# Block products of four feed-forwards: two more raw weight buffers, and rounds of 4, 6, 6, 6 chunks

## The chip, the cores and the metric

The kernel runs on one core of a Trainium2 chip. The metric is the device time of one execution in microseconds; the figure of a kernel is the median of its runs, and less is better. Everything is computed in float32 accuracy: each float32 operand is split into a rounded high part H and a remainder L, and a product takes three matmuls (H by H, H by L, L by H).

## The reference

Two transformer blocks in a row, each of two layers, on one sequence of 512 tokens of width 1024. Each layer holds a mixer (dilated attention, gated linear attention, a latent attention with a short convolution) and one or two gated feed-forwards. The change touches the feed-forwards only:

```python
def swiglu(h, w_gate_up, w_down):
    g, u = jnp.split(h @ w_gate_up, 2, axis=-1)
    return (jax.nn.silu(g) * u) @ w_down
```

Here `h` is 512 x 1024, `w_gate_up` is 1024 x 5632, `w_down` is 2816 x 1024. There are six such feed-forwards in the program.

## The kernel before

A feed-forward (`ffn`, L472) cuts the 2816 hidden columns into 22 chunks of 128 and works through them in rounds. A round computes its chunks (gate, up, silu, product, split into `gH` and `gL`) and then a down phase: for four pairs of output blocks `m`, all chunks of the round times `w_down`, added to the residual `x` by VectorE (`x_add`, L408). Two of the six feed-forwards use plain matmuls (`ffn_up`, L518). The other four, called fast here, are the ones of the change. In them chunks 0 to 3 are plain, and from chunk `FAST` = 4 on each chunk is a block product (`ffn_fast`, L618): the 1024-deep product of one gate and one up column block with two halves of the tokens is done with seven half-size products in place of eight, 84 matmuls of 256 columns a chunk, and five additions of the products on VectorE (L626, `s<-...`), the product of the halves (L648) and the split of the result (`gL`).

The weights of a block product are prepared by a chain (`fast_w`, L582) that runs one chunk ahead. It takes two raw loads of 512 KB (each two DMAs of 256 KB), a left one (rows 0 to 511: `a11`, `a21`) and a right one (rows 512 to 1023: `a12`, `a22`), and makes four sums on GpSimd (L588, tile `sr`, s1 to s4), of which the first needs the right load and the last, s4, is the last reader of the right load. ScalarE casts and VectorE subtracts to split `a11` and the four sums (`swH`, `swL`) and the whole right load (`wh`, `wl`, four buffers).

All raw loads of the program, left, right and those of the plain and the down weights, go into one tag with three buffers:

```python
raw = self.wp.tile([P, kc, n], F32, tag="wraw", name=self.nm("wraw"), bufs=3)
```

The list of loads is fixed in advance (`ffn_specs`, L439), the loader stands four entries ahead of the use (`AHEAD` = 3, `pop_ahead`), and all loads go through SyncE's queue, which issues them in order: a load that waits for its buffer holds those behind it. The order of the instructions on each engine is made by the compiler's scheduler; each engine then runs its list strictly in order. At the end of the plain chunks, `ffn_up` also starts `fast_h` (L545), which makes the sums of the token halves, tiles `ta` and `tb`.

PSUM has three `mm` banks, two `sc` and one `o`, and a bank is given out again when its last reader is done.

Of the kernel before, what the change touches and what calls it, by code (L numbers as in the profile page):

```python
# [8 lines left out]
F32 = mybir.dt.float32  # L9
# [7 lines left out]
P = 128  # L17
S = 512
D = 1024
NC = D // P  # L20
NT = S // P
FF = 2816
# [19 lines left out]
OWN = [("ada", 3)] * 3 + [("adacc", 2)] * 2 + [("lw", 3)] * 3  # L42
FFN_CUTS = ((0, 6), (6, 16))

FAST_CUTS = ((0, 6), (6, 8), (14, 8))
FAST = 4
OWN += [("taH", 1), ("taL", 1), ("tbH", 1), ("tbL", 1)]
HALF = (slice(0, S // 2), slice(S // 2, S))
# [154 lines left out]
class Net:  # L203
# [140 lines left out]
    def wload(self, name, layer, r0, kc, c0, n, own=None):  # L344

        nc = self.nc
        raw = self.wp.tile([P, kc, n], F32, tag="wraw", name=self.nm("wraw"), bufs=3)
        if isinstance(c0, tuple):

            b = n // 2  # L350
            for i in range(2):
                src = self.A[name][layer, r0:r0 + kc * P, c0[i]:c0[i] + b].rearrange("(k p) n -> p k n", p=P)
                nc.sync.dma_start(raw[:, :, i * b:(i + 1) * b], src)
        else:
            src = self.A[name][layer, r0:r0 + kc * P, c0:c0 + n].rearrange("(k p) n -> p k n", p=P)
            nc.sync.dma_start(raw, src)
        if own == "raw":
            return raw
        if own is None:
            H = self.wp.tile([P, kc, n], F32R, tag="wh", name=self.nm("wh"), bufs=4)  # L360
            L = self.wp.tile([P, kc, n], F32R, tag="wl", name=self.nm("wl"), bufs=4)
        else:
            H, L = (self.tile(t, [P, kc, n], F32R, b) for t, b in OWN[2 * own:2 * own + 2])
        self.split(H, L, raw)
        return [(H[:, k], L[:, k]) for k in range(kc)]
# [77 lines left out]
    @staticmethod  # L443
    def ffn_specs(wgu, wdn, l, fast=False):
        for j0, nj in FAST_CUTS if fast else FFN_CUTS:
            for j in range(j0, j0 + nj):
                if fast and j >= FAST:
                    if j == FAST:
                        yield from Net.fast_specs(wgu, l, j)
                    yield from Net.fast_specs(wgu, l, j + 1)  # L450
                elif j % 2 == 0:
                    for part in range(2):
                        for k in range(0, NC, 4):
                            yield wgu, l, k * P, 4, part * FF + j * P, 2 * P
            for m in range(0, NC, 2):
                yield from Net.down_specs(wdn, l, j0, nj, m, fast)

    @staticmethod
    def fast_specs(wgu, l, j):

        return [(wgu, l, k * P, 4, (j * P, FF + j * P), 2 * P, "raw") for k in range(0, NC, 4) if j < FF // P]

    @staticmethod
    def down_specs(wdn, l, j0, nj, m, fast=False):
# [4 lines left out]
    def ffn(self, pre, wgu, wdn, l, coef, norm, begin=None, ada=False, fast=False):  # L469

        with self.phase(4):
            self.g_bufs = 8 if fast else 16  # L472
            for j0, nj in FAST_CUTS if fast else FFN_CUTS:
                last = j0 + nj == FF // P
                gs = []
                for j in range(j0, j0 + nj):
                    if fast and j >= FAST:
                        gs.append(self.ffn_fast(wgu, l, j))
                    elif j % 2 == 0:
                        gs += self.ffn_up(pre, wgu, l, j, fast and j + 2 == FAST)  # L480
                    if j == 0:
                        if begin is not None:
                            with self.tc.issue_after(self.ahead):
                                begin()
                        self.ada_on = True
                if last:
                    self.ada_on = ada
                for m in range(0, NC, 2):
                    specs = list(self.down_specs(wdn, l, j0, nj, m, fast))
                    if last and m == NC - 2:  # L490
                        self.ada_on = False
                        if ada:
                            self.ada_on = True
                            self.until(lambda: self.ada.done)
                            self.ada_on = False
                        self.until(lambda: not self.ada_open)
                        parts = [self.part(*s) for s in specs]
                        for half in range(2):
                            ps = [self.bank(("mm", "sc")[half], [P, S // 2]) for _ in range(2)]
                            self.pairs(ps, parts, gs, HALF[half])  # L500
                            for i in range(2):
                                self.x_add(m + i, ps[i], coef, norm, half)
                            norm.finish(half)
                        norm.wait(0)
                    else:
                        ps = [self.bank(("mm", "sc")[m // 2 % 2], [P, S]) for _ in range(2)]
                        self.pairs(ps, self.parts(specs), gs)
                        for i in range(2):
                            self.x_add(m + i, ps[i], coef, norm if last else None)
# [1441 lines left out]
```

## Time and profile before

| | before |
|---|---|
| median of 3 runs | 3761.65 us (3760.25 to 3763.08) |
| the profiled execution: time, and span of its instructions | 3759.42 us, 3757.6 us |
| mean granted TensorE clock | 0.978 |
| busy share: TensorE matmul, weight load, VectorE, ScalarE, GpSimd | 95%, 84%, 67%, 42%, 18% |
| mean DMA rate over the span | 102 GB/s |

In the rows, PE is TensorE (PEld its weight loads), DVE is VectorE, ACT ScalarE, POOL GpSimd, SP SyncE; `mm<-hH,swH` names the tile written and the tiles read, buffer numbers left out. Idle time stands in square brackets or behind the bar, with the instruction that ended it. The clock column is the share of TensorE's full clock that was granted.

The four fast feed-forwards run their block products at about 1393 to 1680, 2393 to 2680, 2780 to 3068 and 3407 to 3697 us of the span.

### The profile page before, as it was taken

What the parts mean: (1) busy time and instruction counts of PE and PEld (TensorE: products, weight loads), DVE (VectorE), ACT (ScalarE), POOL (GpSimd) and SP (SyncE); (2) the same over time, 40 slices, a digit from 0 to 9 for tenths busy, and PEclk for the clock granted to TensorE, in tenths of its full rate; (3) what the DMA queues carried; (4) which work ended last, traced back from release to release, by engine and by line L of the source; (5) the groups of instructions that cost most, each with busy time, mean ns of one, the idle gap of its engine ahead of it and who ended that gap; (6) DMA issues with size and microseconds to landing.
All of it is one profiled execution on the core that took longest, in us unless ns stands there. A gap on an engine that the chain in (4) does not pass through costs nothing.

```text
span 3757.6 us, 55731 instructions
## 1 busy us (share of the span) xinstructions
PE 3585.0 (95%) x21654; PEld 3168.1 (84%) x21654; DVE 2505.6 (67%) x4331; ACT 1571.0 (42%) x2960; POOL 690.9 (18%) x532
## 2 busy tenths in 40 slices
PE   9999999999999989999999999899989999998998
PEld 7878788888888978888888888788888888887888
DVE  7676667786546676666765478775677566777765
ACT  5545455422236543343222355443443334543433
POOL 3111211000001133230000000342133220013431
PEclk9999999999999989999999999999999999999999
DMA  4122121286432223324764221233313232213232
GB/s 128 57 68 63 51 69 61 84 283 223 152 87 66 75 62 96 101 85 162 264 226 132 75 90 57 73 90 96 112 58 101 90 102 83 76 50 98 79 101 74
DMA packets 402625, 384.98 MB, mean 102 GB/s; under 512 B 19626, under 2 KB 375480, under 8 KB 402360
## 3 DMA queue, kind: packets, MB, share of 16 engines
q1 hardware_dynamic: 402360, 381.42, 32.2%
q8 instruction: 170, 2.79, 0.3%
q14 instruction: 95, 0.78, 0.1%
HBM read 379.26 MB, written 2.10 MB: 101 GB/s over the span
## 4 chain that ended last, share of the span: by engine, by line
PE 76%; DVE 9%; DMA 5%; issue 5%; ACT 3%; POOL 2%; SPq 0%; ACTq 0%; POOLq 0%; DVEq 0%
PE mm L230 46%; PE sc L230 21%; PE o L230 4%; DVE swL L322 3%; PE sm L230 2%; DMA wraw<-in_ffn_w_down 2%; DMA wraw<-in_ffn_w_gu 2%; PE pt L230 2%; DVE wl L322 1%; ACT wh L321 1%; POOL sr L588 1%; DVE s L551 1%; DMA wraw<-in_ffn_w_gate_up 1%; DMA ada<-in_w_ada 1%; DVE s L626 1%
## 5 line engine op out<-in xcount | busy, mean ns | idle before, releaser
L322 DVE TENSOR_TENSOR wl<-wraw,wh 128x1024 fp32r<-128x1024 f32 (+2 forms) x501 | 605.0, 1210 | 438.7 <-ACT wh L321 428.1
L321 ACT CAST wh<-wraw 128x1024 fp32r<-128x1024 f32 (+2 forms) x501 | 508.3, 1019 | 820.3 <-PE mm L230 286.6
L230 PE MATMUL mm<-hL,wh 128*128 128x512 f32 (+1 forms) x1288 | 441.2, 346 | 2.2 <-DVE hL L129 1.8
L230 PE MATMUL mm<-hH,wl 128*128 128x512 f32 (+1 forms) x1288 | 439.6, 346 | 0.0
L230 PE MATMUL mm<-hH,wh 128*128 128x512 f32 (+1 forms) x1288 | 426.8, 348 | 13.3 <-ACT hH L128 11.2
L230 PE MATMUL mm<-wh,hH 128*128 128x512 f32 (+1 forms) x896 | 318.4, 358 | 3.1 <-ACT hH L321 1.7
L230 PE MATMUL mm<-wh,hL 128*128 128x512 f32 (+1 forms) x896 | 316.4, 354 | 0.0
L230 PE MATMUL mm<-wl,hH 128*128 128x512 f32 (+1 forms) x896 | 313.8, 353 | 1.5 <-DVE wl L322 1.5
L230 PEld LDWEIGHTS mm<-hH,wh 128*128 128x128 f32 x1288 | 235.2, 190 | 45.1 <-ACT hH L128 13.1
L230 PEld LDWEIGHTS mm<-hL,wh 128*128 128x128 f32 x1288 | 245.4, 191 | 31.2 <-DVE hL L129 2.2
L322 DVE TENSOR_TENSOR swL<-sr,swH 128x512 fp32r<-128x512 f32 x288 | 262.9, 923 | 12.6 <-ACT swH L321 11.5
L230 PEld LDWEIGHTS mm<-hH,wl 128*128 128x128 f32 x1288 | 245.6, 191 | 29.3
L385 POOL TENSOR_TENSOR rs<-rs,mhalf 128x2 f32<-128x2 f32 (+1 forms) x26 | 22.3, 858 | 1271.8 <-DVE rs L384 1271.8
L230 PE MATMUL sc<-hH,wl 128*128 128x512 f32 (+1 forms) x688 | 237.3, 349 | 0.0
L230 PE MATMUL sc<-hL,wh 128*128 128x512 f32 (+1 forms) x688 | 237.1, 349 | 0.0
L321 ACT CAST swH<-sr 128x512 fp32r<-128x512 f32 x288 | 173.2, 618 | 131.7 <-PE mm L230 79.7
L230 PE MATMUL sc<-hH,wh 128*128 128x512 f32 (+1 forms) x688 | 226.8, 350 | 0.0
L230 PE MATMUL mm<-gH,wh 128*128 128x512 f32 x528 | 208.8, 400 | 12.7 <-ACT wh L321 9.3
L588 POOL TENSOR_TENSOR sr<-wraw,wraw 128x512 f32<-128x512 f32 x72 | 100.9, 1402 | 647.6 <-DMA wraw<-in_ffn_w_gu 382.3
L230 PE MATMUL mm<-gH,wl 128*128 128x512 f32 x528 | 209.8, 398 | 3.9 <-DVE wl L322 3.9
L230 PE MATMUL mm<-hH,swH 128*128 128x256 f32 x576 | 167.8, 293 | 45.8 <-DVE s L626 45.8
L230 PE MATMUL mm<-gL,wh 128*128 128x512 f32 x528 | 208.6, 395 | 0.0
(518 smaller groups left out, 9862.7 us busy)
## 6 DMA issues: line engine op xcount, KB each, us to landing
ada<-in_w_ada SPq DMA_DIRECT2D x144, 512.0 KB
wraw<-in_ffn_w_gu SPq DMA_DIRECT2D x216, 256.0 KB
wraw<-in_ffn_w_down SPq DMA_DIRECT2D x96, 512.0 KB
wraw<-in_ffn_w_gu SPq DMA_DIRECT2D x68, 512.0 KB
wraw<-in_a_w_in SPq DMA_DIRECT2D x128, 256.0 KB
wraw<-in_ffn_w_gate_up SPq DMA_DIRECT2D x52, 512.0 KB
wraw<-in_ffn_w_down SPq DMA_DIRECT2D x48, 384.0 KB
wraw<-in_ffn_w_gate_up SPq DMA_DIRECT2D x72, 256.0 KB
```

Of the source, the lines that this page charges most:

```text
L230: self.nc.tensor.matmul(out, lhsT, rhs, **kw)
L321: self.nc.scalar.copy(H, src)
L322: return self.nc.vector.tensor_tensor(out=L, in0=src, in1=H.bitcast(F32), op=ALU.subtract).ins
L385: self.pow = self.nc.gpsimd.tensor_tensor(out=rs, in0=rs, in1=self.mhalf[:, :rs.shape[1]], op=ALU.pow).ins
L551: add, sub = (lambda o, a, b, e=e, op=op: e.tensor_tensor(out=o, in0=a, in1=b, op=op) for e, op in ((nc.gpsimd, ALU.add), (nc.vector, ALU. ...
L588: nc.gpsimd.tensor_tensor(out=o, in0=a, in1=b, op=op)
L626: add = lambda o, a, b: nc.vector.tensor_tensor(out=o, in0=a, in1=b, op=ALU.add)
```

## The change

- `FAST_CUTS`: the rounds of a fast feed-forward are chunks 0-3, 4-9, 10-15, 16-21 in place of 0-5, 6-13, 14-21. The first round then holds plain chunks only, and its down phase stands between them and the first block product. A down phase of six chunks takes its weights in two loads of three chunks a pair `m`, one of four chunks in one load of four.
- Right loads go to a tag of their own, `fr`, with two buffers; left loads stay in `wraw`.
- `g_bufs` falls from 8 to 6: the two tags `gH`, `gL` lose two buffers each, 8 KB a partition in all, which is what the two `fr` buffers take.
- The two loads of chunk 4 keep their place in the list of loads, right behind the plain chunks.

```diff
-FAST_CUTS = ((0, 6), (6, 8), (14, 8))
+FAST_CUTS = ((0, 4), (4, 6), (10, 6), (16, 6))
...
-        raw = self.wp.tile([P, kc, n], F32, tag="wraw", name=self.nm("wraw"), bufs=3)
+        if own == "right":
+            raw = self.tile("fr", [P, kc, n], F32, 2)
+        else:
+            raw = self.wp.tile([P, kc, n], F32, tag="wraw", name=self.nm("wraw"), bufs=3)
...
-        if own == "raw":
+        if own in ("left", "right"):
             return raw
...
                 if fast and j >= FAST:
-                    if j == FAST:
-                        yield from Net.fast_specs(wgu, l, j)
                     yield from Net.fast_specs(wgu, l, j + 1)
                 elif j % 2 == 0:
...
+                    if fast and j + 2 == FAST:
+                        yield from Net.fast_specs(wgu, l, FAST)
...
-        return [(wgu, l, k * P, 4, (j * P, FF + j * P), 2 * P, "raw") for k in range(0, NC, 4) if j < FF // P]
+        return [(wgu, l, k * P, 4, (j * P, FF + j * P), 2 * P, side) for k, side in ((0, "left"), (4, "right"))
+                if j < FF // P]
...
-            self.g_bufs = 8 if fast else 16
+            self.g_bufs = 6 if fast else 16
```

What this does to the order of the instructions is shown at three places of the first fast feed-forward. Each name carries the number of its tile; a tile with a higher number was asked for later.

**Place 1**, SyncE's queue in the middle of the second round of block products: six loads in a row before, left and right in turn, all in `wraw`.

```order
L353 DMA wraw_2577_14163<-in_ffn_w_gate_up 128x4x128 x2
L353 DMA wraw_2578_14166<-in_ffn_w_gate_up 128x4x128 x2
L353 DMA wraw_2605_14306<-in_ffn_w_gate_up 128x4x128 x2
L353 DMA wraw_2606_14309<-in_ffn_w_gate_up 128x4x128 x2
L353 DMA wraw_2633_14449<-in_ffn_w_gate_up 128x4x128 x2
L353 DMA wraw_2634_14452<-in_ffn_w_gate_up 128x4x128 x2
```

The same place now, in a round of six:

```order
L356 DMA wraw_2674_14676<-in_ffn_w_gate_up 128x4x128 x2
L356 DMA wraw_2681_14728<-in_ffn_w_gate_up 128x4x128 x2
L356 DMA wraw_2709_14871<-in_ffn_w_gate_up 128x4x128 x2
L356 DMA fr_2682_14731<-in_ffn_w_gate_up 128x4x128 x2
L356 DMA fr_2710_14874<-in_ffn_w_gate_up 128x4x128 x2
L356 DMA wraw_2737_15014<-in_ffn_w_gate_up 128x4x128 x2
L356 DMA fr_2738_15017<-in_ffn_w_gate_up 128x4x128 x2
L356 DMA wraw_2765_15157<-in_ffn_w_gate_up 128x4x128 x2
L356 DMA fr_2766_15160<-in_ffn_w_gate_up 128x4x128 x2
```

Before, each load waits for the buffer of the third one ahead of it, so that the right load `wraw_2606` takes the buffer of the left load `wraw_2577`, which `fast_w` is still reading. Now a right load waits for the right load two chunks earlier, and a left one for the left one three chunks earlier.

**Place 2**, VectorE within a round: before, the split `wl` of a right load stands in the list of every chunk, between the splits `swL` of the sums and the additions (L626) that TensorE waits for.

```order
L626 TENSOR_TENSOR s_2602_14300<-mm_2604_14302,s_2600_14298 128x256
L322 TENSOR_TENSOR swL_2648_14525<-sr_2637_14459,swH_2647_14524 128x512
L648 TENSOR_TENSOR s_2602_14300<-s_2602_14300,s_2601_14299 128x512
L322 TENSOR_TENSOR wl_2669_14624<-wraw_2606_14309,wh_2668_14623 128x1024
L322 TENSOR_TENSOR swL_2651_14548<-sr_2642_14484,swH_2650_14547 128x512
L626 TENSOR_TENSOR s_2628_14441<-sc_2646_14511,s_2628_14441 128x256
L322 TENSOR_TENSOR gL_2625_14434<-s_2602_14300,gH_2624_14433 128x512
L322 TENSOR_TENSOR swL_2655_14581<-sr_2643_14486,swH_2654_14580 128x512
```

Now, at the second chunk of a round:

```order
L630 TENSOR_TENSOR s_2704_14863<-sc_2715_14895,s_2704_14863 128x256
L322 TENSOR_TENSOR wl_2773_15189<-fr_2710_14874,wh_2772_15188 128x1024
L322 TENSOR_TENSOR swL_2724_14947<-sr_2713_14881,swH_2723_14946 128x512
L322 TENSOR_TENSOR gL_2701_14856<-s_2678_14722,gH_2700_14855 128x512
L322 TENSOR_TENSOR swL_2727_14970<-sr_2718_14906,swH_2726_14969 128x512
L630 TENSOR_TENSOR s_2704_14863<-sc_2722_14933,s_2704_14863 128x256
L322 TENSOR_TENSOR swL_2731_15003<-sr_2719_14908,swH_2730_15002 128x512
L630 TENSOR_TENSOR s_2705_14864<-mm_2708_14867,s_2704_14863 128x256
```

The row `wl_2773`, of the fifth right load of this round, is the only split of a right load in the list from the first chunk of the round to the third; those of the first four stand just ahead of the `x` rows of the down phase before the round and among them, and that of the sixth at the end of the fourth chunk.

**Place 3**, ScalarE at the change from the plain chunks to what follows. `s<-mm` at L535 (L539 now) is the silu that frees a gate bank; `wh_2424` is the right load of chunk 4.

```order
L321 CAST wh_2424_13344<-wraw_2409_13301 128x1024
L321 CAST swH_2430_13371<-sr_2423_13333 128x512
L321 CAST swH_2434_13388<-sr_2422_13331 128x512
L321 CAST swH_2438_13411<-sr_2426_13348 128x512
L321 CAST swH_2442_13434<-sr_2427_13350 128x512
L321 CAST swH_2467_13538<-wraw_2410_13304 128x512
L321 CAST taH_2412_13313<-s_2436_13401 128x512
L321 CAST tbH_2414_13315<-s_2437_13406 128x512
L321 CAST taH_2412_13313<-s_2444_13447 128x512
L321 CAST tbH_2414_13315<-s_2445_13452 128x512
L535 ACTIVATE s_2450_13504<-mm_2404_13294 128x512
L535 ACTIVATE s_2453_13511<-mm_2405_13295 128x512
```

Now:

```order
L321 CAST wh_2411_13306<-wraw_2410_13304 128x1024
L321 CAST swH_2446_13423<-sr_2434_13360 128x512
L321 CAST swH_2450_13446<-sr_2435_13362 128x512
L321 CAST wh_2414_13312<-wraw_2413_13310 128x1024
L321 CAST taH_2416_13319<-s_2444_13413 128x512
L321 CAST tbH_2418_13321<-s_2445_13418 128x512
L321 CAST taH_2416_13319<-s_2452_13459 128x512
L321 CAST swH_2483_13668<-wraw_2466_13532 128x512
L321 CAST tbH_2418_13321<-s_2453_13464 128x512
L321 CAST wh_2423_13329<-wraw_2422_13327 128x1024
L539 ACTIVATE s_2458_13516<-mm_2404_13294 128x512
L321 CAST taH_2416_13319<-s_2456_13497 128x512
L539 ACTIVATE s_2461_13523<-mm_2405_13295 128x512
```

The cast of the right load is gone from ahead of the silu (it stands behind it now), and the casts of three down weights of the new first down phase stand ahead of it (`wh_2411`, `wh_2414`, `wh_2423`); VectorE's list has their splits ahead of the gate product (L536, L540 now) in the same way, at all four fast feed-forwards, and at two of them that of a fourth. `swH_2483` is the split of the left load of chunk 5, whose buffer is that of the second down weight.

## Rows read from the trace of the kernel before

**Rows 1.** The page: busy time of each engine.
```profile
PE 3585.0 (95%) x21654; PEld 3168.1 (84%) x21654; DVE 2505.6 (67%) x4331; ACT 1571.0 (42%) x2960; POOL 690.9 (18%) x532
```
**Rows 2.** TensorE's waits, one fast feed-forward each: total us, times, longest.
```profile
PE mm L230 <- DVE s L626: 11.2, 7, 3.0
...
PE mm L230 <- DVE s L626: 11.1, 8, 3.7
...
PE mm L230 <- DVE s L626: 11.4, 6, 3.2
...
PE mm L230 <- DVE s L626: 12.0, 7, 3.3
```
**Rows 3.** Stretches: length, busy PE, PEld, DVE, ACT, POOL; PEclk, DMA share, GB/s.
```profile
1450.00:1680.00 230.00, 214.30 (x1532) 200.84 (x1531) 153.73 (x215) 91.52 (x159) 89.03 (x60) 0.99 0.31 92
2455.00:2680.00 225.00, 210.46 (x1511) 198.02 (x1510) 150.12 (x211) 89.84 (x156) 85.71 (x58) 0.98 0.31 92
2848.00:3068.00 220.00, 203.94 (x1483) 192.76 (x1481) 150.02 (x211) 89.30 (x157) 83.69 (x56) 0.98 0.30 89
3470.00:3697.00 227.00, 211.23 (x1512) 198.63 (x1511) 152.46 (x212) 90.73 (x159) 84.44 (x57) 0.98 0.30 91
...
1493.20:1496.20 3.00, 3.00 (x16) 3.00 (x16) 3.00 (x5) 1.41 (x3) 1.39 (x1) 0.50 0.08 24
```
**Rows 4.** Waits of all engines, 1460 to 1540 us (a round of eight).
```profile
POOL sr L588 <- DMA wraw<-in_ffn_w_gate_up: 22.2, 5, 5.5
DVE wl L322 <- ACT wh L321: 16.7, 5, 6.3
...
PE mm L230 <- DVE s L626: 7.2, 4, 2.9
```
**Rows 5.** Timelines of SP, POOL, ACT, DVE, PE at one chunk: start, us, instruction.
```profile
1480.41 0.37 SPq L353 DMA_DIRECT2D wraw<-in_ffn_w_gate_up  x1
...
1485.90 1.30 POOL L588 TENSOR_TENSOR sr<-wraw,wraw 128x512 f32<-128x512 f32 x1 [5.52 <-DMA wraw<-in_ffn_w_gate_up]
...
1485.82 1.06 ACT L321 CAST wh<-wraw 128x1024 fp32r<-128x1024 f32 x1 [5.60 <-DMA wraw<-in_ffn_w_gate_up]
...
1486.91 1.38 DVE L322 TENSOR_TENSOR wl<-wraw,wh 128x1024 fp32r<-128x1024 f32 x1 [4.71 <-ACT wh L321]
...
1492.15 0.39 PE L230 MATMUL mm<-hH,swH 128*128 128x256 f32 x1 [2.85 <-DVE s L626]
```
**Rows 6.** Chunk starts, busy time between first and last, and `swL` min/median/max ns.
```profile
L631 ACT COPY s<-mm x8: 365/370/373, 1460.5 to 1536.9; 128x256 f32<-128x256 f32 x8
...
1460.50:1536.90 76.40, 69.17 (x566) 68.27 (x564) 58.93 (x86) 33.53 (x65) 39.84 (x27) 0.98 0.27 77
...
L322 DVE TENSOR_TENSOR swL<-sr,swH x29: 674/680/1778, 1461.3 to 1538.6; 128x512 fp32r<-128x512 f32 x29
...
L322 DVE TENSOR_TENSOR swL<-sr,swH 128x512 fp32r<-128x512 f32 x29 | 26.4, 916 | 0.3 <-ACT swH L321 0.2
```
**Rows 7.** A down phase of eight chunks: VectorE's `x` additions, and busy time.
```profile
L416 DVE TENSOR_TENSOR x<-mm,x 128x512 f32<-128x512 f32 x4 | 2.7, 689 | 2.9 <-PE mm L230 2.9
...
1545.00:1595.00 50.00, 49.15 (x233) 40.50 (x232) 22.39 (x24) 13.40 (x15) 5.95 (x4) 1.00 0.41 126
```
**Rows 8.** Change from plain chunks to block products: TensorE's waits, busy time, VectorE by form.
```profile
PE mm L230 <- ACT s L535: 5.7, 1, 5.7
PE sc L230 <- DVE s L536: 2.6, 1, 2.6
...
1386.00:1406.00 20.00, 11.67 (x65) 11.10 (x64) 17.69 (x25) 7.94 (x14) 11.20 (x8) 0.66 0.09 27
2393.00:2413.00 20.00, 11.94 (x72) 10.96 (x71) 19.98 (x27) 8.98 (x16) 11.98 (x9) 0.74 0.09 27
...
L322 DVE TENSOR_TENSOR swL<-sr,swH 128x512 fp32r<-128x512 f32 x4 | 6.2, 1613 | 1.8 <-ACT swH L321 1.8
...
L322 DVE TENSOR_TENSOR wl<-wraw,wh 128x1024 fp32r<-128x1024 f32 x1 | 1.8, 1786 | 0.4 <-ACT wh L321 0.4
```

## The prediction

> **What bounds the kernel now.** I read the page first: TensorE is busy 95% of the span, VectorE 67% and the others less [rows 1]. So an edit pays only where TensorE now waits, or where it runs at a lower granted clock. Its waits come next, one fast feed-forward at a time: the largest row is the same in all four, matmuls on an `mm` bank that wait for VectorE's additions (L626), 11.2, 11.1, 11.4 and 12.0 us, 45.7 us in 28 waits [rows 2]. Busy time by stretch adds the clock: from the second round on it is 0.98 or 0.99 [rows 3], and (1 - clock) times length gives 2.3 + 4.5 + 4.4 + 4.5 = 15.7 us (the column has two digits, so a few us either way). Right behind a wait of 2.85 us [rows 5], for instance, the clock is 0.50 [rows 3], 1.2 in place of 2.4 GHz, although TensorE is busy again. Waits and clock together, 61.4 us, are all that this stage can give back.
>
> Why are the additions late? VectorE isn't full. From the first to the last chunk start of a round of eight, 7 chunks in 76.4 us or 10.9 each, TensorE is busy 9.9 us a chunk, VectorE 8.4 and GpSimd 5.7 [rows 6]. In that round VectorE sits idle for 16.7 us, nearly all of its idle time, in front of five splits `wl` of right loads, waiting for ScalarE's cast `wh`; GpSimd waits for the load itself, 22.2 us [rows 4]. One chunk in order of time shows the chain [rows 5]. The next pair of raw loads is issued from 1480.41 on, when the last sum s4 has released a buffer; `wh` and the first sum start only at 1485.82 and 1485.90, 5.4 us later. VectorE stands 4.71 us in front of `wl`, with splits of sums and an addition behind it whose inputs are there; it then works them off, and TensorE's matmul starts only at 1492.15, after 2.85 us of waiting for an addition. So the loop is s4, load, cast, split, and VectorE's list in order makes a late load a late bank.
>
> **The change, part by part.**
>
> *Two raw buffers more.* SyncE's list (place 1) shows right loads in `fr`: each now waits for the right load two chunks earlier, so a load of 5.4 us has about a chunk of 9.9 us in which to land. The wait for the load leaves the loop. VectorE's list (place 2) shows more: of a round's six splits of right loads four stand at the down phase before it, so the row in front of which VectorE stands idle today comes once between the first chunk and the fourth. That one, the fifth, can still be late: its buffer comes free with the s4 of the third chunk, which GpSimd makes while the first is multiplied. Without the idle time VectorE needs 8.4 us of 9.9, so it catches up by 1.5 us a chunk.
> I can't read from a trace without the change how many waits stay. Bounds: all go (45.7 us), or none does (0). Nearest row: three fifth splits a feed-forward, 12 in all, can still give a wait like today's, 45.7/28 = 1.6 us, which would leave 19.6 us; but those loads have a lead that today's haven't. Between 19.6 and 0 left I take two thirds off, -30.5 us, and two thirds of the clock, -10.5 us.
>
> *Rounds of 4, 6, 6, 6.* The matmuls are as many in columns. Successions of block product to block product: 1 + 7 + 7 = 15 before, 5 + 5 + 5 = 15 now. Turns from block products to a down phase: three before and three now. Each fast feed-forward gets eight `x` additions more, 0.69 us each [rows 7], 5.5 us of VectorE, 22 us in all; in a down phase VectorE is busy 22.4 of 50 us [rows 7], and that TensorE work hides them. If it did not, they would cost up to 22 us; half of VectorE's time being free excludes most of it. Four more splits of the same bytes in smaller pieces hide there too. Two buffers of `gH` and `gL` less: a chunk's split needs the buffer of a chunk six earlier, which the down phase has finished reading a whole chunk's 9.9 us before. Nothing.
>
> *The change from plain chunks to the rest (place 3).* Today TensorE stands here for the silu that frees a gate bank, 5.7 us, and for the gate product, 2.6 us; VectorE is busy 17.7 to 20.0 of 20 us and the clock is 0.66 and 0.74 [rows 8]. Here VectorE is the bound. Now the first down phase stands in TensorE's list in place of the first block product, and it needs the same gate bank, so the wait stays. In VectorE's list the split of the right load leaves the stretch ahead of the gate product and at least three splits of down weights enter it: two more, 1.79 us each as the one there took [rows 8], 3.6 us. Against it the right load of chunk 4 doesn't wait for a `wraw` buffer any more, and 1.8 us for which VectorE now stands before the first sums' splits [rows 8] can go. Net 1.8 us a feed-forward, +7.2 us. Bounds: 0, if the splits fill idle time only, and 3.6 us of wait with as much again at half clock, 7.2 us each, 29 us in all.
>
> Sum: -30.5 - 10.5 + 7.2 = -33.8 us. The profiled execution took 3759.42 us (span 3757.6), so 3725.6; the median of the runs lies 2.2 us above it, so 3728 us.
>
> **The rivals.**
>
> *VectorE becomes the bound (half the gain).* Its splits of sums take 680 ns at the median, but 916 on average and 1778 at most [rows 6], and the long ones lie beside GpSimd's sums. With the load's pause gone, GpSimd and VectorE work at once for more of a chunk. The price: 4.1 such splits a chunk, from 916 to 1778 ns at worst, add 3.6 us to 8.4, 12.0 a chunk, over TensorE's 9.9. It decides from +1.5 us a chunk; at +2.5, today's 10.9, nothing is won. Half way, 10.4 us, half of the 41.0 us stays: 3761.65 - 20.5 + 7.2 = 3748 us. Against it: the same work and the same GpSimd time a chunk are in the 8.4 already, and four of six `wl` leave the stretch. The Trainium skill, SBUF — State Buffer, section "Who interferes with whom", has a rule for this: a VectorE instruction with two SBUF inputs and a GpSimd instruction that reads SBUF share a read interface, and the one that comes second is blocked until the first ends. By that rule all 5.7 us of GpSimd could be added to VectorE's chunk. The trace agrees that some is, as the 1778 ns shows, but the average of 916 says that most splits pass unhindered.
>
> *The wait stays in every chunk (the change doesn't do what it says).* If the buffer of a right load came free only just ahead of its use, ScalarE and VectorE would stand before the same cast as today. Speaking for it: it is still s4 that frees it. Against: s4 of two chunks earlier, and VectorE's list (place 2). Then only the +7.2 is left, or nothing: 3762 to 3769 us.
>
> *The start of the first down phase eats the gain (slower).* One mechanism: place 3 puts the split `swH_2483` of chunk 5's left load ahead of the silu, and that load's buffer is free only when VectorE has split the second down weight. Then ScalarE stands for a whole load, 5.4 us [rows 5], behind VectorE's two more splits, 3.6 us: 9.0 us at every fast feed-forward, and as long again at half clock as today, 20 us at 0.66 to 0.74 or some 6 us [rows 8]. 15 us times four is 60 us, against 41.0 won: 3761.65 + 19 = 3781 us. It decides from about 10 us a feed-forward. Against it: between the second down weight and `swH_2483` ScalarE's list holds three casts of `ta` and `tb` (place 3), each behind VectorE's work for it in a stretch where VectorE has no idle time, so most of the 5.4 us is covered.
>
> **How the numbers follow.** Most waits go: 0.60, own range 3700 (all 61.4 us, nothing at the start) to 3748 (a third of it, and the 7.2). VectorE bound: 0.12. Wait stays: 0.13. The start eats the gain: 0.15. A change under 0.2%, 7.5 us, can't be told from none by these runs. The first two cases are faster, 0.72; the third is the same, 0.13; the last is slower, 0.15. The range goes from 3701, which leaves a few in a hundred of the first case below, to 3769, which takes in the second and third and leaves the last out.
>
> **What would show it.** TensorE's waits for L626 fall from 11 to 12 us a fast feed-forward to about 4; the clock from the second round on is 0.99 or 1.00; a chunk within a round takes 10.0 to 10.3 us in place of 10.9; VectorE's wait for `wh` inside a round falls from five stands to one, and GpSimd no longer waits for DMA there. If VectorE binds, its busy time a chunk is above 9.9 us. If the start eats the gain, TensorE's waits between the last plain chunk and the first down phase are over 15 us, with ScalarE waiting for a DMA in front of the silu. The prediction is wrong above all if GpSimd's sums, started earlier, delay VectorE by more than the load did, or if the scheduler's order needs VectorE earlier than it can be there.

## The result, and the profile after

The changed kernel takes 3720.27 us (median of 4 runs, 3717.76 to 3721.55) against 3762.36 us of the kernel before beside it (4 runs): a ratio of 0.9887, interval 0.987 to 0.9904. The forecast was 3728 us. The profiled execution took 3721.55 us, its span is 3719.7 us. The total came out nearly as forecast, the parts did not.

The page's busy row answers to [rows 1]. TensorE is busy 16.6 us less, VectorE 68 us more, with only 48 instructions more:

```profile
PE 3568.4 (96%) x21606; PEld 3155.4 (85%) x21606; DVE 2573.7 (69%) x4379; ACT 1573.6 (42%) x2976; POOL 696.8 (19%) x532
```

Below, a stage is the time from the last matmul of a fast feed-forward's plain chunks to the end of its last down phase, so that the same work stands in it in every kernel. First the stages of the kernel before, by stretch (columns as in [rows 3]), first and last of four and their sum:

```profile
1386.20:1727.70 341.50, 314.51 (x2090) 288.93 (x2089) 217.79 (x305) 130.83 (x218) 102.60 (x69) 0.97 0.31 93
...
3405.00:3747.70 342.70, 317.52 (x2118) 291.36 (x2116) 223.14 (x311) 133.09 (x224) 107.95 (x73) 0.97 0.27 82
sum 1360.60, PE 1257.58 PEld 1155.23 DVE 886.91 ACT 526.92 POOL 422.29; mean PE 314.39 PEld 288.81 DVE 221.73 ACT 131.73 POOL 105.57
```

The same view of the changed kernel, all four, their sum, and four shorter stretches that the text comes to:

```profile
1385.80:1709.90 324.10, 309.09 (x2078) 284.68 (x2076) 230.93 (x315) 130.71 (x221) 109.88 (x69) 0.98 0.32 95
2372.80:2704.20 331.40, 310.44 (x2076) 286.60 (x2076) 239.57 (x319) 130.14 (x221) 105.05 (x71) 0.96 0.32 94
2758.00:3086.80 328.80, 309.50 (x2078) 284.98 (x2076) 237.63 (x317) 130.49 (x221) 102.47 (x69) 0.97 0.31 92
3375.90:3709.40 333.50, 311.15 (x2093) 287.53 (x2093) 238.28 (x321) 131.61 (x226) 104.39 (x71) 0.97 0.28 83
sum 1317.80, PE 1240.17 PEld 1143.79 DVE 946.41 ACT 522.95 POOL 421.79; mean PE 310.04 PEld 285.95 DVE 236.60 ACT 130.74 POOL 105.45
...
1417.80:1471.55 53.75, 50.55 (x419) 49.56 (x417) 43.82 (x59) 25.14 (x48) 28.16 (x20) 1.00 0.30 89
1461.46:1471.55 10.09, 8.49 (x70) 8.12 (x68) 9.72 (x11) 6.09 (x12) 4.82 (x4) 1.00 0.42 131
1472.20:1475.00 2.80, 2.80 (x14) 2.80 (x15) 2.80 (x5) 0.72 (x2) 0.64 (x1) 0.50 0.10 18
...
2707.80:2714.60 6.80, 5.38 (x23) 5.09 (x24) 4.98 (x13) 2.73 (x6) 0.25 (x1) 0.50 0.25 70
```

The stages are 42.8 us shorter (1360.6 to 1317.8). Length less PE busy is TensorE's idle time: 103.0 before, 77.6 now, so 25.4 us of the gain are waits and 17.4 us are busy time. Only part of the busy time is half clock: taken in stretches of 2 us, (1 - clock) times busy time adds up to 31.5 us in the four stages before and 26.1 us now, some 5 us less, and the mean granted clock of the whole execution is 0.978 in both kernels. What the other 12 us of busy time are stays open. About 5 us are lost again outside: behind the first three of these feed-forwards TensorE stands 1.8 to 1.9 us for the sum of squares (`nacc`), which it didn't before; behind the second it then works at 0.50 for 6.8 us (last row).

Which waits went? First the rows of the kernel before for its first stage (total us, times, longest) that [rows 2] and [rows 8] don't show:

```profile
PE mm L230 <- ACT wh L321: 3.6, 4, 2.1
...
PE o L230 <- ACT wh L321: 1.2, 2, 1.0
PE mm L230 <- DVE wl L322: 1.0, 2, 0.8
...
PE o L230 <- DVE wl L322: 0.7, 1, 0.7
```

and of the changed kernel, each stage's two largest:

```profile
PE mm L230 <- DVE s L630: 8.6, 8, 2.1
PE mm L230 <- ACT s L539: 5.7, 1, 5.7
...
PE mm L230 <- ACT s L539: 10.5, 1, 10.5
PE mm L230 <- DVE s L630: 9.2, 7, 2.4
...
PE mm L230 <- ACT s L539: 9.3, 2, 8.0
PE mm L230 <- DVE s L630: 8.8, 7, 2.2
...
PE mm L230 <- DVE s L630: 11.1, 7, 3.3
PE mm L230 <- ACT s L539: 9.9, 1, 9.9
```

| TensorE's waits in the four stages, us | before | after |
|---|---|---|
| for additions (L626, L630) | 45.7 | 37.7 |
| for `wh`, `wl` of down weights and right loads (6.5, 5.0, 5.9, 4.3) | 21.7 | 0 |
| where the plain chunks end (8.3, 8.1, 7.8, 7.8; now the L539 rows) | 32.0 | 35.4 |
| other | 3.6 | 4.5 |

So the waits that the forecast was about fell by 8.0 us, and those that it priced at nothing, at the turns between block products and down phases, went altogether.

What it said of the loads is there. Waits of all engines in one round, 1417 to 1480 us, beside [rows 4]:

```profile
DVE wl L322 <- ACT wh L321: 4.5, 4, 1.6
...
POOL sr L592 <- DMA fr<-in_ffn_w_gate_up: 3.0, 1, 3.0
```

GpSimd's 22.2 us of waiting for a load became 3.0, VectorE's 16.7 us in front of `wl` 4.5 (in 63 us in place of 80). But TensorE still waits for additions. From the first chunk start to the last of this round a chunk takes 10.75 us (53.75 over five; 10.55 and 10.44 in the next two rounds) in place of 10.9, and VectorE is busy 8.8 us of it, where it was 8.4. The end of that round in order of time (start, us, engine) shows why:

```profile
1465.73 1.78 DVE L652 TENSOR_TENSOR s<-s,s 128x512 f32<-128x512 f32 x1
1467.43 1.77 DVE L322 TENSOR_TENSOR swL<-sr,swH 128x512 fp32r<-128x512 f32 x1
1469.12 0.41 DVE L630 TENSOR_TENSOR s<-sc,s 128x256 f32<-128x256 f32 x1
1469.46 1.64 DVE L322 TENSOR_TENSOR swL<-sr,swH 128x512 fp32r<-128x512 f32 x1
...
1471.96 0.41 DVE L630 TENSOR_TENSOR s<-o,s 128x256 f32<-128x256 f32 x1
...
1465.34 1.61 POOL L592 TENSOR_TENSOR sr<-wraw,fr 128x512 f32<-128x512 f32 x1 [5.56 <-DVE swL L322]
1467.03 1.62 POOL L592 TENSOR_TENSOR sr<-sr,wraw 128x512 f32<-128x512 f32 x1
1469.28 1.27 POOL L592 TENSOR_TENSOR sr<-wraw 128x512 f32<-128x512 f32 x1 [0.63 <-DVE swL L322]
1471.23 1.60 POOL L592 TENSOR_TENSOR sr<-fr,sr 128x512 f32<-128x512 f32 x1 [0.68 <-POOL sr L592]
...
1472.09 0.50 PE L230 MATMUL mm<-hH,swH 128*128 128x256 f32 x1 [2.05 <-DVE s L630]
```

Three VectorE instructions that take 0.68 us elsewhere take 1.64 to 1.78 here, each beside one of GpSimd's sums, and end 0.55 us or so behind it (1465.73 + 1.78 = 1467.51; the sum ends at 1466.95). VectorE is busy 9.72 of 10.09 us in that chunk, TensorE stands 2.05 us and then works at a clock of 0.50. This is a reading of one trace; the experiments test it.

### The profile page after: what moved, and what is told of

It reads as the page before. It is cut to its first block, busy times and chain, and to the rows that moved or that the text cites. A ratio compares the mean times of both kernels' runs of the same rounds, so it can differ in the third digit from the quotient of the medians.

```text
span 3719.7 us, 55676 instructions
## 1 busy us (share of the span) xinstructions
PE 3568.4 (96%) x21606; PEld 3155.4 (85%) x21606; DVE 2573.7 (69%) x4379; ACT 1573.6 (42%) x2976; POOL 696.8 (19%) x532
## 4 chain that ended last, share of the span: by engine, by line
PE 79%; DVE 10%; issue 4%; DMA 3%; ACT 3%; POOL 1%; SPq 0%; ACTq 0%; DVEq 0%; POOLq 0%
PE mm L230 49%; PE sc L230 23%; PE o L230 4%; DVE swL L322 3%; PE sm L230 2%; DVE wl L322 2%; PE pt L230 1%; DVE s L630 1%; DVE gL L322 1%; ACT wh L321 1%; DMA wraw<-in_ffn_w_down 1%; DMA ada<-in_w_ada 1%; DMA fr<-in_ffn_w_gu 1%; DVE s L652 1%; DVE s L555 1%
## 5 line engine op out<-in xcount | busy, mean ns | idle before, releaser
L322 DVE TENSOR_TENSOR wl<-wraw,wh 128x1024 fp32r<-128x1024 f32 (+3 forms) x445 | 534.2, 1203 | 293.2 <-ACT wh L321 289.4
L321 ACT CAST wh<-wraw 128x1024 fp32r<-128x1024 f32 (+3 forms) x445 | 438.8, 988 | 650.3 <-PE mm L230 269.0
L322 DVE TENSOR_TENSOR swL<-sr,swH 128x512 fp32r<-128x512 f32 x288 | 281.5, 990 | 10.1 <-ACT swH L321 9.3
L230 PE MATMUL mm<-gH,wh 128*128 128x512 f32 x528 | 208.4, 401 | 38.0 <-ACT s L539 35.4
L592 POOL TENSOR_TENSOR sr<-wraw,fr 128x512 f32<-128x512 f32 x72 | 116.2, 1615 | 566.0 <-DVE swL L322 280.2
L230 PEld LDWEIGHTS mm<-wh,hH 128*128 128x128 f32 x896 | 185.9, 208 | 24.0 <-issue 3.3
```

Of the source, the lines that this page charges most:

```text
L230: self.nc.tensor.matmul(out, lhsT, rhs, **kw)
L321: self.nc.scalar.copy(H, src)
L322: return self.nc.vector.tensor_tensor(out=L, in0=src, in1=H.bitcast(F32), op=ALU.subtract).ins
L592: nc.gpsimd.tensor_tensor(out=o, in0=a, in1=b, op=op)
```

## The experiments

Each is timed beside the kernel before; the ratio is to that, with its interval. Line numbers shift by a few from kernel to kernel: L626, L627, L630, L631 and L633 are the same additions.

| rounds | right loads | sums | `ta`, `tb` | median us | ratio |
|---|---|---|---|---|---|
| 4, 6, 6, 6 | own ring | GpSimd | before the silu | 3720.27 | 0.9887 (0.987 to 0.9904): the change |
| 4, 6, 6, 6 | one ring | GpSimd | " | 3731.62 | 0.9906 (0.9892 to 0.9919) |
| 6, 6, 5, 5 | own ring | GpSimd | " | 3719.71 | 0.9873 (0.986 to 0.9887) |
| 6, 6, 5, 5 | one ring | GpSimd | " | 3736.03 | 0.9921 (0.9908 to 0.9935) |
| 4, 6, 6, 6 | left own | GpSimd | " | 3689.66 | 0.9792 (0.9779 to 0.9806) |
| 4, 6, 6, 6 | own ring | GpSimd | behind | 3708.85 | 0.9844 (0.9831 to 0.9858) |
| 4, 6, 6, 6 | left own | GpSimd | behind, queued | 3679.54 | 0.9771 (0.9758 to 0.9785) |
| 4, 6, 6, 6 | own ring | two of four left out | before the silu | 3642.10 | 0.9669 (0.9656 to 0.9682) |
| 4, 6, 6, 6 | own ring | VectorE | " | 3647.24 | 0.9684 (0.9671 to 0.9697) |
| 6, 8, 8 | one ring | VectorE | as before | 3674.35 | 0.9755 (0.9742 to 0.9769) |
| 4, 6, 6, 6 | own ring | VectorE | behind, queued | 3622.66 | 0.9619 (0.9606 to 0.9632) |
| 4, 6, 6, 6 | left own | VectorE | behind, queued | 3631.66 | 0.9646 (0.9633 to 0.9659) |
| 4, 6, 6, 6 | own ring | VectorE, with those of `ta`, `tb` | behind, queued | 3613.62 | 0.9593 (0.958 to 0.9606) |

**The rounds alone, and their shape.** Three kernels: the rounds without the ring; the ring with rounds of another shape; that shape without the ring. (The ring with rounds of eight is missing: its 8 KB a partition come from the four `gH`, `gL` buffers that a round of eight uses.)

```diff
-        if own == "right":
-            raw = self.tile("fr", [P, kc, n], F32, 2)
-        else:
-            raw = self.wp.tile([P, kc, n], F32, tag="wraw", name=self.nm("wraw"), bufs=3)
+        raw = self.wp.tile([P, kc, n], F32, tag="wraw", name=self.nm("wraw"), bufs=3)
```

> The changed kernel with its rounds of 4, 6, 6, 6 and six g buffers, but all raw loads, the right ones too, in the one ring of three wraw buffers as before. Theory 'ring': the gain comes from the right loads having a ring of their own, because the down weights then land before the turn into a down phase (TensorE's waits there for wh and wl, 21.7 us in all four feed-forwards before, none in the changed kernel). Then most of the 42 us are lost: 3750 to 3765 us, with 4 us or more of waits for wh and wl in each feed-forward and 11 us for the additions. Rival 'shape': the gain comes from the rounds, since the first down phase fills the change from plain chunks and no round is longer than six. Then 3718 to 3735 us without the ring.

```diff
-FAST_CUTS = ((0, 4), (4, 6), (10, 6), (16, 6))
+FAST_CUTS = ((0, 6), (6, 6), (12, 5), (17, 5))
```

> The changed kernel with rounds of 6, 6, 5, 5 chunks: right loads keep their ring of two, but chunks 4 and 5 stand behind the plain chunks again, as in the kernel before, and the first down phase comes after them. 'Ring': 3712 to 3730 us, the waits for wh and wl at the turns stay under 1 us a feed-forward. 'Shape': 3740 to 3760 us.

> Rounds of 6, 6, 5, 5 chunks with all raw loads in the one ring of three: no ring of their own, no down phase between the plain chunks and the first block product, six g buffers. Against the kernel before only the two rounds of eight are cut into three of five and six. Theory 'short rounds': TensorE's waits for the additions start only at about the third chunk of a round, so shorter rounds have fewer of them: 20 or fewer such waits in place of 28, and 3728 to 3742 us. Rival 'first down phase': what the run with the rounds of 4, 6, 6, 6 alone gained came from the down phase moved ahead of chunk 4; then 3752 to 3768 us here.

Both shapes do most of it without the ring: 0.9906 and 0.9921. So 'ring' as the whole cause fell, and the down phase ahead of chunk 4 isn't it either: the intervals of the two shapes overlap, with the ring and without it. What they share is short rounds, with the smaller down loads and the six `gH`, `gL` buffers that go with them, which were not tested apart. TensorE's waits with the rounds alone, first and last stage, and its stages' sum by stretch:

```profile
PE mm L230 <- DVE s L627: 5.9, 5, 1.8
...
PE o L230 <- ACT wh L321: 2.4, 3, 2.0
PE mm L230 <- ACT s L645: 2.2, 2, 1.1
...
PE mm L230 <- DVE s L627: 6.9, 5, 1.7
```

```profile
sum 1328.00, PE 1240.60 PEld 1133.90 DVE 893.67 ACT 526.56 POOL 418.21; mean PE 310.15 PEld 283.47 DVE 223.42 ACT 131.64 POOL 104.55
```

The additions cost 5.9 + 6.4 + 6.6 + 6.9 = 25.8 us in 20 waits, against 45.7 us in 28; with 6, 6, 5, 5 and one ring they are 16.2 us in 13. They don't lie evenly. In the round of eight of the kernel before, whose chunks start between 1460.5 and 1536.9 [rows 6], all four lie in its middle; the first and the last in order of time:

```profile
1479.63 0.39 PE L230 MATMUL mm<-hH,swH 128*128 128x256 f32 x1 [0.67 <-DVE s L626]
...
1518.08 0.38 PE L230 MATMUL mm<-hH,swH 128*128 128x256 f32 x1 [2.00 <-DVE s L626]
```

The first round of six with the rounds alone has two:

```profile
1436.10 0.39 PE L230 MATMUL mm<-hH,swH 128*128 128x256 f32 x1 [1.08 <-DVE s L627]
...
1448.84 0.39 PE L230 MATMUL mm<-hH,swH 128*128 128x256 f32 x1 [1.75 <-DVE s L627]
```

A likely reason, not tested by itself: a round's first chunks are prepared in the down phase ahead of it, and its last have no right load behind them that the round itself needs. A shorter round loses its middle. It doesn't explain the changed kernel, where the longest wait of the first two rounds, 2.05 us each, stands right behind the start of the last chunk.

The second thing to see is VectorE's busy time: 893.67 us here, 946.41 us with the ring, for the same list of work. The ring takes away the waits for `wh` and `wl` that the rounds left, 14.7 of 21.7 us, and most of those for the silu of a block product (L645), 12.6 us to 2.4. The waits for additions, which it was meant to end, rise again from 25.8 to 37.7 us, and with 6, 6, 5, 5 from 16.2 to 32.0. That fits sums and splits that now run at the same time, as in the timeline above. In sum the ring is worth 0.2% with these rounds (the intervals overlap) and 0.5% with 6, 6, 5, 5.

**Which loads get the ring.** `if own == "left":` in place of `"right"`.

> The changed kernel with the tags exchanged: left loads have the ring of two, right loads share the ring of three with the plain and down weights. If what counts is that the late release of a right load (by the last sum, s4) no longer holds up a down weight, most of the gain goes: 3738 to 3758 us, waits for wh and wl at the turns are back. If only the number of buffers counts: 3715 to 3726 us, no difference from the changed kernel beyond 0.2%.

Neither: 30.6 us faster than the change. So it isn't only the number of buffers, and the late release of right loads isn't what counts: with the right loads back in the down weights' ring, no stage shows a wait for `wh` or `wl` either. Its waits for additions are 30.3 us, those for the silu where the plain chunks end 25.2, and VectorE's busy time in the stages is 923.9 us, between the two above. With GpSimd out of the way (below) the order of the two is the other one, 3622.66 against 3631.66 us. So the 30 us most likely hang on where GpSimd's sums fall beside VectorE's work (the work for `ta` and `tb` was moved too in those two kernels); which place makes them stays open.

**GpSimd's sums.** In one kernel two of the four sums a chunk are left out, in the other VectorE makes all four:

```diff
-        s2 = tt(s1, a11, ALU.subtract)
-        s4 = tt(a12, s2, ALU.subtract)
-        both("S2", s2)
-        both("S4", s4)
+        both("S2", s1)
+        both("S4", s3)
```

> The changed kernel without two of GpSimd's four sums a chunk (s2 and s4 are left out, s1 and s3 take their places; all casts, splits and matmuls stay). Theory 'GpSimd holds VectorE up': the waits for additions that are left (37.7 us) come from VectorE's splits that take 1.7 us in place of 0.7 beside a sum; with half the sums VectorE's busy time in the four feed-forwards falls from 1015 us by 60 us or more, the waits to under 20 us, and the time to 3680 to 3700 us. Rival 'VectorE's own list': VectorE has too much work of its own at the end of a round, the down weights' splits above all; then the waits stay over 30 us and the time is 3708 to 3722 us.

```diff
-            nc.gpsimd.tensor_tensor(out=o, in0=a, in1=b, op=op)
+            nc.vector.tensor_tensor(out=o, in0=a, in1=b, op=op)
```

> The changed kernel with all four sums a chunk made by VectorE in place of GpSimd. If GpSimd's sums cost VectorE about as much as they would cost it to make them itself (four times 0.69 us a chunk against some 4 splits a chunk that take 1 us longer), the time is the same within 0.3%: 3710 to 3730 us, with splits that take 0.68 us throughout. Rival: most of VectorE's splits pass GpSimd unhindered, so that 2.7 us more a chunk make VectorE the bound in every chunk: over 3760 us.

Both are far below the lower bound of either theory: 3642.10 and 3647.24 us, some 75 us under the change. The first leaves out work, so its time shows only what the waits hang on. With all sums on VectorE, five chunks of the first round and the stages' sum, by stretch:

```profile
1414.00:1464.40 50.40, 50.40 (x429) 50.40 (x429) 47.40 (x84) 26.77 (x50) 0.00 (x0) 1.00 0.33 99
...
sum 1241.50, PE 1211.11 PEld 1123.75 DVE 935.89 ACT 524.61 POOL 8.87; mean PE 302.78 PEld 280.94 DVE 233.97 ACT 131.15 POOL 2.22
```

VectorE's instructions in those chunks (ns, min/median/max), a split and a sum:

```profile
L322 DVE TENSOR_TENSOR swL<-sr,swH x21: 679/684/693, 1414.9 to 1464.2; 128x512 fp32r<-128x512 f32 x21
...
L592 DVE TENSOR_TENSOR sr<-sr,wraw x5: 681/684/685, 1417.1 to 1459.6; 128x512 f32<-128x512 f32 x5
```

TensorE has no idle time in the round. No split of a sum takes over 693 ns, where [rows 6] had 1778. And VectorE, which has 263 instructions more in the stages, is busy 10.5 us less than in the change. 263 times 0.684 us is 180 us; so the 413 us of GpSimd's work that went (421.8 less the 8.9 left) had cost VectorE some 190 us. The waits for additions, 45.7 and 37.7 us, are gone from all four stages. How much of the 73 us comes from VectorE's freed time, and how much from sums that are ready sooner (0.68 us each in place of 1.27 to 1.62), these two kernels don't separate.

The Trainium skill, SBUF — State Buffer, section "Who interferes with whom", states what the timeline above shows: of a VectorE instruction with two SBUF inputs and a GpSimd instruction that reads SBUF the second is blocked until the first ends. The trace agrees in the three instructions shown: each starts behind a sum and ends some 0.55 us behind it, and the additions, which have one input in PSUM, take 0.41 us beside one. The Trainium skill, GPSIMD Engine Reference, section "4.1 Engine selection", puts a two-input operation on GpSimd at about twice VectorE's time. Here a sum takes 1.27 to 1.62 us against 0.68, 1.9 to 2.4 times as long.

**The kernel before with the same move.** One line changed in the kernel before, its rounds and its one ring kept.

> The kernel before, with nothing but its four sums a chunk moved from GpSimd to VectorE. Theory: GpSimd's hold on VectorE made most of the waits of the kernel before, and the ring and the rounds only moved them; then this comes within 1% of the changed kernel with the same move (3647.2 us): 3650 to 3685 us. Rival: the late right load is a wait of its own (ring of three, load, cast, split), which stays whoever makes the sums: over 3700 us, with VectorE still standing 15 us or more a round for the cast of the right load.

3674.35 us, 0.9755: more than twice the gain of the change, from one word. TensorE's two largest waits in its first stage, and two waits of VectorE from 1450 to 1535 us, a round of eight, beside [rows 4]:

```profile
PE mm L230 <- ACT wh L321: 5.5, 3, 2.3
PE mm L230 <- ACT s L535: 2.2, 1, 2.2
...
DVE wl L322 <- ACT wh L321: 5.9, 3, 3.5
...
DVE sr L588 <- DMA wraw<-in_ffn_w_gate_up: 4.7, 5, 1.9
```

No wait for additions there, 3.1 us in all four stages, with the ring of three and rounds of eight. The late right load went with them, though the ring of three stayed: 22.2 us of waiting for it became 4.7, and VectorE's 16.7 us in front of `wl` 5.9. The rival expectation (a wait of its own, over 3700 us, 15 us or more a round) fell. So this run doesn't tell the late load from GpSimd's hold on VectorE, since faster sums also release the load sooner. The changed kernel does: there the ring had taken the wait for the load away, and 37.7 us of waits for additions stayed until the sums left GpSimd. TensorE's waits for `wh` and `wl` are left, 17.9 us in four stages. With ring and rounds they go, and the time falls by 27 us more, to 3647.24.

**Where the plain chunks end.** `ta` and `tb` are made behind the silu of the last plain chunks, in the first down phase:

```diff
-            turned = self.spawn(self.fast_h(h))
...
-            self.until(lambda: turned.done and ready.done)
+            self.until(lambda: ready.done)
...
             out.append(self.g_split(g))
+        if ahead:
+            self.turned = self.spawn(self.fast_h(h))
```

> The changed kernel with the chain that makes ta and tb (fast_h) started behind the silu and product of the last plain chunks, so that its subtractions and splits stand beside the first down phase. Theory: TensorE stands 5.7 to 10.5 us a feed-forward for that silu (35.4 us in all) because VectorE's and ScalarE's work for ta and tb stands ahead of it; then the waits go and with them half of the half clock behind them: 3680 to 3695 us. Rival: VectorE is short of time in this whole stretch, so the wait moves to the split of the last plain chunks (gH, gL) or to ta and tb at the first block products: 3712 to 3726 us.

3708.85 us, 11 us better, between the two: the silu's wait went, but TensorE now stands 10.7 us for `wl` of the first down weights and 8.8 us for the product, since the scheduler still puts the subtractions for `ta` ahead of them. So the next kernels also queue VectorE's part of it behind the last plain split (`with self.tc.issue_after(plain):`).

> The kernel with the ring of two for left loads (3689.7 us), and the chain for ta and tb started behind the last plain chunks, with its VectorE work queued behind their last split, so that it stands beside the first down phase. Theory: the 25.2 us that TensorE still stands for the silu there go, and a few us of half clock: 3655 to 3670 us. Rival: VectorE can't finish ta and tb in that down phase, and TensorE stands for them or for the down weights' splits instead: 3682 to 3695 us.

3679.54 us, 10 us better, again between the two: the waits for the silu are gone, 33.9 us for additions stay, and 12.4 us for `x` additions are new.

**Both moves.**

> The changed kernel (ring of two for right loads) with all four sums a chunk on VectorE (3647.2 us so), and the work for ta and tb started behind the last plain chunks, VectorE's part queued behind their last split. Theory: the 25.9 us of waits for the silu that are left there go, and some half clock: 3614 to 3628 us. Rival: VectorE, over 9 us busy in 9.9 now, can't finish ta and tb beside the first down phase: 3640 to 3652 us.

> As the run before last (sums on VectorE, ta and tb behind the plain chunks), but the left loads have the ring of two and the right ones share the ring of three. If the 30 us between the two kinds of ring came from where GpSimd's sums fall beside VectorE's splits, nothing of them is left: within 0.3% of that run. If they came from the order of the loads, this is 15 to 30 us faster than it.

("That run" is the one above it, with the ring for right loads.) 3622.66 us, as the theory said; with the ring for left loads 3631.66 us, 0.3% slower. The first by stretch, the first stage and the sum, and TensorE's two largest waits in that stage:

```profile
1386.50:1690.10 303.60, 300.52 (x2078) 279.37 (x2076) 236.37 (x391) 129.93 (x220) 5.95 (x4) 1.00 0.34 99
...
sum 1216.70, PE 1204.18 PEld 1119.71 DVE 949.54 ACT 520.92 POOL 23.79; mean PE 301.05 PEld 279.93 DVE 237.39 ACT 130.23 POOL 5.95
```

```profile
PE sc L230 <- DVE s L633: 1.1, 1, 1.1
PE mm L230 <- ACT s L651: 1.1, 1, 1.1
```

12.5 us of idle time in four stages at a clock of 1.00. The eight additions for `ta` and `tb` on VectorE too:

> The kernel with the sums of the weights on VectorE and the work for ta and tb behind the plain chunks (3622.7 us), with the eight additions for ta and tb on VectorE too, so that GpSimd has no work in the four feed-forwards. Theory: each of these additions still lengthens a VectorE instruction beside it; the few waits that are left in the first down phase go: 3610 to 3619 us. Rival: nothing in this stage waits for VectorE any more but some 12 us, most of it elsewhere than beside those additions, and eight additions more (5.5 us) stand in VectorE's list: 3619 to 3630 us, no difference.

3613.62 us, 9 us better with intervals that touch: the theory's number; that it is these additions is likely, not shown apart. This beats both kernels, by 152 us and 107 us.

## Why the prediction was nearly right

The size was right, most of it for other reasons than those given: waits for additions and half clock gave much less than forecast, and the turns, which stand in the sum with nothing, gave 21.7 us. That these cancel to within 8 us is luck.

- *"Waits and clock together, 61.4 us, are all that this stage can give back."* Wrong. With run after run taken away the stages gave 144 us (1360.6 to 1216.7). The figure left out the waits at the turns (21.7 us), those where the plain chunks end (32.0) and the rest of TensorE's busy time: 53 us of it went in all, where 15.7 were counted.
- *Two thirds of the additions' waits, -30.5.* Measured -8.0, and not by the ring: the rounds alone make -19.9, the ring adds 11.9 again. The mechanism began as described: right loads land early, GpSimd doesn't wait for them, VectorE hardly stands in front of `wl` (four short stands, where one was forecast). The step that failed is *"without the idle time VectorE needs 8.4 us of 9.9, so it catches up"*. The 8.4 us had been measured with VectorE pausing while GpSimd waited too; side by side its busy time in the stages rises by 59.5 us, 52.7 of them over the kernel with the rounds alone, which has the same list of work.
- *The half clock, -10.5.* Mis-sized: in the stages half clock costs 31.5 us before and 26.1 now, some 5 us less, and behind the first 60 us of each stage, where the forecast looked for it, 2 us less (17.5 to 15.6). Behind 10 of the 13 longest waits for additions that are left (1.70 to 3.30 us) the clock falls to half again. Busy time fell by 17.4 us all the same, most of it not by the clock. The run at a clock of 1.00 does this work in 1204 us, 53 us less than before and 36 us less than now.
- *Rounds: as many successions, as many turns, "Nothing".* This step failed most: the rounds alone bring 0.94%. Equal counts don't make equal waits: those for additions lay in the middle of the long rounds, and fell by 19.9 us with shorter ones. The turns cost 21.7 us before, 14.7 with the rounds alone, and nothing with two raw buffers more, whichever loads have them.
- *Place 3, +7.2.* 32.0 to 35.4 us of waits: the sign was right, the size about half. The prediction's rows are those of the first stage; in the second and fourth TensorE stood here for `tbH` and `tbL` before, and stands for the silu now. Whether two more splits make the difference no run shows.
- *"VectorE becomes the bound", given 0.12.* This rival was the true one in kind: the row with splits of 1778 ns beside an average of 916 was its evidence, and the text set it aside because most splits passed unhindered. An average of 916 over 680 is a third more time on the largest group of that engine's instructions, and should have been priced as such. VectorE isn't the bound throughout, as the rival had it: it is busy 8.8 us of a chunk of 10.75, and nearly all of it only ahead of the last chunk (9.72 of 10.09). That was enough to take most of the additions' gain; the unpriced turns gave as much back.
- *"The wait stays in every chunk"* and *"the start eats the gain"* didn't come: the waits lie in one to four chunks of a round, and no stage stands over 10.5 us at its start.

## What to carry to other kernels

Price an engine's busy time anew when a change lets it run beside another: look at the spread of one instruction's duration (680 to 1778 ns), not at the idle time that is left. Before a buffer is added for a late load, move the neighbour's work and see whether the load is still late: here one word was worth more than twice the ring and the rounds. And waits that are not those a change is made for, at the turns and where a stage starts, belong in the sum.

## What the hardware showed that was not expected

VectorE makes the same sum in 0.68 us that takes GpSimd 1.27 to 1.62 us, and 413 us of such work in four stages cost VectorE some 190 us, where making the sums itself took it 180: handing them to GpSimd relieved VectorE of nothing. Behind waits of 2.05 us (here) and 1.9 us (`nacc`) the rows show a clock of 0.50. Behind another wait of 2.05 us, to 1657.34 in the changed kernel, the clock stays at 1.00, so the length of the one wait doesn't settle it. In the stages of the kernel with both moves, where no wait is over 1.2 us, they show 1.00 throughout.
